# Two changes of order and of PSUM use in the FFN of a two-layer trunk on Trainium2

## The chip, the core and the metric

One core of a Trainium2 chip (trn2) runs the whole step as one program. The time is the device time of that core in microseconds, the median over repeated runs. TensorE (PE) does the products, VectorE (DVE), ScalarE (ACT) and GpSimd (POOL) what stands between them, SyncE (SP) issues the loads.

## The reference

`reference()` is one inference step of a trunk of two layers. Each layer is a half-step SwiGLU FFN, a token mixer (three head groups) and a second half-step FFN. The change lies in the FFN alone:

```python
def _ffn_half(x, mod, slot, w1, w3, w2, g, b):
    h = _modulate(x, mod[:, 3 * slot], mod[:, 3 * slot + 1])
    f = (jax.nn.silu(h @ w1) * (h @ w3)) @ w2
    return _residual_post_norm(x, f, mod[:, 3 * slot + 2], FFN_RES, g, b)
```

There are 640 tokens (128 of context, 512 latent), a model width of 1024 (8 tiles of 128 rows, called d0 to d7 here) and a hidden width of 2816 (22 tiles). Everything is float32.

## The kernel before

The activations lie transposed: a tile holds 128 features by 640 tokens. A float32 product is made of three fast ones: every operand is split into a high part (`hh`, `gh`, `wh`) and the small rest (`hl`, `gl`, `wl`), and high by high, high by low and low by high are summed in PSUM.

**One FFN** (function `ffn`; four calls, called FFN 1 to 4 here) goes over the 22 hidden tiles in six chunks of 3, 3, 3, 4, 4 and 4. The first three hidden tiles are computed plainly. Each of the other 19 is a `Pair`: the columns of w1 and of w3 for this hidden tile are stacked as a matrix of two by two blocks, the activations as another (features 0 to 511 and 512 to 1023, tokens 0 to 319 and 320 to 639), and the product is taken by a seven-product scheme, p1, p2, p4, p6, p7, p5, p3 in this order, each of 12 matmuls of 128x320 (L847) into one PSUM bank. The operands that are sums of blocks come from two places: of the activations (`t1` to `t4`) once per FFN, of the weights (`s1` to `s4`) on POOL for each pair (`combine`, L259). After a product's matmuls, `prod` calls `slot()`, which runs the follow-up steps put into the list `later`; a step that returns another step has that one run at the next slot. So a result of a product is read one product later or more. The steps: ACT copies p1 into `pm` (L895), DVE adds p2, p6, p7, p4, p5 and p3 to it in turn (`op`, L858), ACT takes the silu (L863, L877), DVE multiplies the two halves (L858, L881), and `hi` and `lo` split the product into `gh` (ACT, L886) and `gl` (DVE, L891). For the last pair of a chunk the first half of the tokens is split earlier, by `half` (L477, L478).

**The end of a chunk.** When the pairs are done, the remaining steps in `later` are issued, and the chunk's part of the product with w2 begins: eight feature tiles, each 3 matmuls for each hidden tile of the chunk and each part of the tokens (256 and 384 columns, L485), into `o`. Two tiles are begun (`begun`) with all hidden tiles but the last, whose `gh` is not there yet; `end_begun` then adds the last. `rows` does the others, and for each `resid` (DVE, L610) adds the result to the residual `x`, and `each()` may issue a step of the modulation vectors (`scr`, DVE L460, in FFN 1 to 3 only). The last chunk goes to `rows_norm` instead, which also takes the layer norm.

**PSUM.** Two buffers are double (two banks, `dbl`), four are single (`bank`). Buffers of a kind are used in turn, and the first matmul into one waits for the last reader of what it held.

**The weights** come through `Stream`, in the order in which `get` asks for them. A job is a half of a tile's load: SP loads the raw tile into one of two buffers (`wr`, L243), ACT makes the high part (`wh`, L299), DVE or POOL the low part (`wl`, L306). `get` converts ahead, as many jobs as fit in SLOTS (6) buffers, and the low part of a job is issued with `lows()` when the next job is converted. So the place of a `wl` in DVE's order is set by the calls of `get` around it, and a raw buffer comes free, and its next load can start, when the `wl` that reads it has been done.

What sets the work's order on each engine is then the order in which the Python code issues instructions.

```python
                while later:
                    slot()
                begun = []
                for d in range(2):
                    w = ws.get()
                    p = dbl("o") if d == 0 else [bank("o"), bank("o")]
```

Of the kernel before, what the change touches and what calls it, by code (L numbers as in the profile page):

```python
# [7 lines left out]
F32 = mybir.dt.float32  # L8
# [97 lines left out]
def trunk_kernel(tc, I, O):  # L106
# [3 lines left out]
    with ExitStack() as es:  # L110
# [520 lines left out]
        def rows(acts, n, begun, each):  # L631

            end_begun(begun, acts, n)
            for d in range(KD):
                if d < len(begun):
                    p = begun[d][1]
                else:
                    w = ws.get()
                    p = dbl("o")
                    mm(p, w, acts, 0, n)  # L640
                    mm(p, w, acts, 1, n)
                resid(p, d, None)
                each()

# [185 lines left out]
        class Pair:  # L830


            def __init__(self, h, tb, last):
                self.last = last
                self.b11, self.b21, self.b22 = ([[a[:, c] for a in h[k]] for k in ks]
                                                for ks, c in ((range(4), slice(0, HN)), (range(4, 8), slice(0, HN)),
                                                              (range(4, 8), slice(HN, T))))
                self.t1, self.t2, self.t3, self.t4 = (Quarter(tb, i) for i in range(4))
                self.m, self.sl = u(pe_, f"pm{uid()}"), None

            def out(self):
                self.gh, self.gl = u(pe_, f"gh{uid()}", F32R), u(pe_, f"gl{uid()}", F32R)
                return self.gh, self.gl

            def mms(self, out, w, b, k):
                for i, (a, c) in enumerate(((0, 0), (0, 1), (1, 0))):
                    PE.matmul(out[:, :HN], w[a][:, k, :], b[k][c], start=k == 0 and i == 0, stop=k == 3 and i == 2)  # L847

            def prod(self, out, b, post=None, w=None):
                w = w or ws.get()  # L850
                for k in range(4):
                    self.mms(out, w, b, k)
                slot()
                if post:
                    later.append(post)
# [1 line left out]
            def op(self, o, a, b, f):  # L857
                V.tensor_tensor(out=o, in0=a, in1=b[:, :HN], op=f)  # L858

            def c11(self, p2):  # L860
                self.sl = u(pe_, f"sl{uid()}")
                self.op(self.sl[:, LO], self.m[:, LO], p2, ALU.add)
                return lambda: S.activation(self.sl[:, LO], self.sl[:, LO], AF.Silu) and None  # L863

            def gate1(self):
                self.op(self.g[:, LO], self.g[:, LO], self.sl, ALU.mult)
                return self.half if self.last else None

            def half(self):
                split(self.gh[:, LO], self.gl[:, LO], self.g[:, LO])  # L870

            def c12(self, p3):
                self.op(self.sl[:, HI], self.m[:, LO], p3, ALU.add)
                return self.silu2

            def silu2(self):
                S.activation(self.sl[:, HI], self.sl[:, HI], AF.Silu)  # L877
                return self.gate2

            def gate2(self):  # L880
                V.tensor_tensor(out=self.g[:, HI], in0=self.g[:, HI], in1=self.sl[:, HI], op=ALU.mult)  # L881
                return self.hi

            def hi(self):
                c = HI if self.last else slice(0, T)
                S.copy(self.gh[:, c], self.g[:, c])  # L886
                return self.lo

            def lo(self):
                c = HI if self.last else slice(0, T)  # L890
                V.tensor_tensor(out=self.gl[:, c], in0=self.g[:, c], in1=self.gh[:, c].bitcast(F32), op=ALU.subtract)  # L891

            def start(self):
                p1, p2 = bank("p1"), bank("p2")
                self.prod(p1, self.b11, lambda: S.copy(self.m[:, LO], p1[:, :HN]) and None)  # L895
                self.prod(p2, self.b21, lambda: self.c11(p2))

            def run(self, mods, begun=False):
                m, op = self.m, self.op
                if not begun:  # L900
                    self.start()
                mods(0)
                p45 = dbl("p4")
                p4, p5 = p45[:, 0, :], p45[:, 1, :]
                self.prod(p4, self.t4)
                p6 = bank("p6")
                self.prod(p6, self.t2, lambda: op(m[:, LO], m[:, LO], p6, ALU.add))
                mods(1)
                p7 = bank("p7")

                def u3():
                    op(m[:, HI], m[:, LO], p7, ALU.add)
                    self.g = u(pe_, f"gf{uid()}")
                    op(self.g[:, LO], m[:, HI], p4, ALU.subtract)
                    return self.gate1
                self.prod(p7, self.t3, u3)

                def u4():
                    op(self.g[:, HI], m[:, HI], p5, ALU.add)
                    op(m[:, LO], m[:, LO], p5, ALU.add)  # L920
                self.prod(p5, self.t1, u4)
                mods(2)
                p3 = bank("p3")
                self.prod(p3, self.b22, lambda: self.c12(p3))

            def run_first(self, mods, other, ts):

                m, op = self.m, self.op
                self.start()
                mods(0)  # L930
                other.start()
                p3 = bank("p3")
                self.prod(p3, self.b22, None, ws.get(4))
                w22 = ws.get(0)
                p45, p6, p7 = dbl("p4"), bank("p6"), bank("p7")
                p4, p5 = p45[:, 0, :], p45[:, 1, :]
                wq = [ws.get(0), ws.get(0), ws.get(2), w22]
                for k in range(4):
                    for o, w, b in zip((p5, p7, p6, p4), wq, (self.t1, self.t3, self.t2, self.t4)):
                        self.mms(o, w, b, k)  # L940
                    mods(k)
                    next(ts, 0)
                slot()

                def post():
                    self.g = u(pe_, f"gf{uid()}")
                    op(m[:, LO], m[:, LO], p6, ALU.add)
                    op(m[:, HI], m[:, LO], p7, ALU.add)
                    op(self.g[:, LO], m[:, HI], p4, ALU.subtract)
                    op(self.g[:, HI], m[:, HI], p5, ALU.add)  # L950
                    op(m[:, LO], m[:, LO], p5, ALU.add)
                    later.append(self.gate1)
                    return self.c12(p3)
                later.append(post)

        LO, HI = slice(0, HN), slice(HN, T)

# [58 lines left out]
        def ffn(l, f, h, first, nmod, nvec, norm, scale_x, tb, ts):  # L1016
# [29 lines left out]
            for ci, (j0, j1) in enumerate(CHUNKS):  # L1046
# [44 lines left out]
                while later:  # L1091
                    slot()
                begun = []
                for d in range(2):
                    w = ws.get()
                    p = dbl("o") if d == 0 else [bank("o"), bank("o")]
                    for half in range(2):
                        for k in range(n - 2 if ci == 0 else n - 1):
                            mmk(part(p, half), w, gs, half, k, k, n)
                    begun.append((w, p, n - 1))  # L1100
# [911 lines left out]
        for l in range(DEPTH):  # L2012
            for f in range(2):
                for j0, j1 in CHUNKS:
                    for j in range(j0, j1):
                        tw = [I["w13"][l, f, j, :, wi] for wi in range(2)]
                        if j < NC:
                            for wi in range(2):
                                ws.tile(tw[wi], (KD, P), "m" if 2 * j + wi == NOPEN else None)
                            continue  # L2020
                        r = ws.pair(*tw)
                        for nm in BLOCKS:
                            ws.block(nm, r)
                    for d in range(KD):
                        ws.tile(I["w2"][l, f, d, :, j0:j1], (j1 - j0, P), "t" if j1 == NFF and d >= KD - NTAIL else None)
                if f == 1:
                    break
                for i in (0, 1, 3):
                    ws.tile(I["wint"][l, i], (KD, P))
                for gi in range(2):  # L2030
                    for hf in range(2):
                        ws.tile(I["winn"][l, gi, hf], (4, 256), None if gi + hf else "m")
                for i in (2, 4, 5, 6, 7, 8, 9, 10, 11):
                    ws.tile(I["wint"][l, i], (KD, P))
                ws.tile(I["wqup"][l], (6, P))
                ws.tile(I["wkvup"][l], (4, P))
                for d in range(KD):
                    ws.tile(I["wo"][l, d], (KD, P), "t" if d >= KD - NTAIL else None)
# [161 lines left out]
```

## Time and profile before

| what | value |
|---|---|
| median of 3 runs | 2693.86 us (2693.51 to 2696.27) |
| the profiled execution's own time | 2705.26 us |
| its span, first to last instruction | 2703.3 us |
| mean granted TensorE clock | 0.976 |
| busy: PE, DVE, ACT, POOL | 95%, 77%, 43%, 46% of the span |

The profile is of one execution. The span is from its first to its last instruction, and its own time stands 2 us above it. A share of busy time is a mean over the whole span. The trace's timeline gives each instruction's start and length, and in brackets how long its engine was idle before it and what ended that. The four FFNs lie at about 50 to 505, 945 to 1372, 1425 to 1843 and 2280 to 2675 us.

### The profile page before, as it was taken

To read this page: it belongs to the slowest core of one execution; us is meant where nothing else is said; L and a number is where in the kernel's file an instruction comes from. 1 tells how busy PE (TensorE), PEld (TensorE's weight loads), DVE (VectorE), ACT (ScalarE), POOL (GpSimd) and SP (SyncE) were. 2 spreads that over 40 slices of the span, in tenths; PEclk is the share of its full clock that TensorE was granted. 3 is DMA by queue.
4 is the path that set the end of the run, shared out by engine and by line. 5 is a ranking of instruction groups with operands and counts; after the bars stand their busy time and mean duration, and the time that the engine had idled before them with its cause. 6 is when DMAs were issued, how large, how long until landed. Compare 5 with 4: busy or idle time off the path is not lost. (4 is left out here: it accounts for less than half of the span.)

```text
span 2703.3 us, 49877 instructions
## 1 busy us (share of the span) xinstructions
PE 2555.0 (95%) x18662; PEld 2453.0 (91%) x18662; DVE 2072.3 (77%) x3759; ACT 1175.9 (43%) x2596; POOL 1244.0 (46%) x973
## 2 busy tenths in 40 slices
PE   7999999899999999999989999998998999999997
PEld 6999999888778999999989999998887798999997
DVE  6599889856764879988987998898476558777776
ACT  5233333545575533333353333334545745334333
POOL 2345445522444554544555454454233456435545
PEclk9999999999999999999989999998999999999998
DMA  7333332354344223333222333323543331222222
GB/s 273 116 98 101 111 97 83 117 152 136 91 130 156 71 96 100 103 101 109 68 83 84 112 103 101 110 87 108 158 134 98 103 114 40 82 82 87 79 86 71
DMA packets 130545, 285.89 MB, mean 106 GB/s; under 512 B 16832, under 2 KB 34560, under 8 KB 129664
## 3 DMA queue, kind: packets, MB, share of 16 engines
q1 hardware_dynamic: 130304, 282.70, 33.2%
q8 instruction: 148, 2.42, 0.4%
q14 instruction: 93, 0.76, 0.1%
HBM read 254.95 MB, written 8.81 MB: 98 GB/s over the span
## 5 line engine op out<-in xcount | busy, mean ns | idle before, releaser
L306 DVE TENSOR_TENSOR wl<-wr,wh 128x512 fp32r<-128x512 f32 (+1 forms) x524 | 518.3, 1003 | 74.1 <-ACT wh L299 72.5
L299 ACT CAST wh<-wr 128x512 fp32r<-128x512 f32 (+1 forms) x570 | 333.3, 607 | 479.4 <-DMA wr<-in_w 296.9
L485 PE MATMUL o<-gh,wh 128*128 128x256 f32 (+1 forms) x1408 | 439.5, 312 | 19.4 <-ACT gh L886 11.7
L485 PE MATMUL o<-gl,wh 128*128 128x256 f32 (+1 forms) x1408 | 439.0, 312 | 1.8 <-DVE gl L478 0.3
L485 PE MATMUL o<-gh,wl 128*128 128x256 f32 (+1 forms) x1408 | 436.7, 310 | 0.0
L847 PE MATMUL p<-hh,wh 128*128 128x320 f32 x1216 | 378.4, 311 | 16.8 <-DVE pm L858 16.8
L847 PE MATMUL p<-hl,wh 128*128 128x320 f32 x1216 | 378.2, 311 | 6.2 <-DVE hl L1010 6.2
L847 PE MATMUL p<-hh,wl 128*128 128x320 f32 x1216 | 378.1, 311 | 0.0
L259 POOL TENSOR_TENSOR ws<-wr 128x512 f32<-128x512 f32 x76 | 111.5, 1468 | 545.8 <-DMA wr<-in_w 482.8
L299 ACT CAST wh<-ws 128x512 fp32r<-128x512 f32 x304 | 185.9, 621 | 361.6 <-PE p L847 153.4
L306 POOL TENSOR_TENSOR wl<-ws,wh 128x512 fp32r<-128x512 f32 x152 | 241.3, 1591 | 193.6 <-ACT wh L299 193.1
L610 DVE SCALAR_TENSOR_TENSOR x<-o,gat,x 128x128 f32<-128x128 f32 (+2 forms) x404 | 192.9, 524 | 139.6 <-PE o L485 136.6
L485 PEld LDWEIGHTS o<-gh,wh 128*128 128x128 f32 x1408 | 267.8, 190 | 23.0 <-ACT gh L886 14.5
L485 PEld LDWEIGHTS o<-gl,wh 128*128 128x128 f32 x1408 | 268.1, 190 | 6.7 <-DVE gl L891 4.8
L485 PEld LDWEIGHTS o<-gh,wl 128*128 128x128 f32 x1408 | 267.9, 190 | 0.0
L847 PEld LDWEIGHTS p<-hh,wh 128*128 128x128 f32 x1216 | 229.9, 189 | 19.0 <-issue 18.9
L847 PEld LDWEIGHTS p<-hl,wh 128*128 128x128 f32 x1216 | 230.0, 189 | 7.4 <-DVE hl L1010 7.4
L847 PEld LDWEIGHTS p<-hh,wl 128*128 128x128 f32 x1216 | 230.0, 189 | 0.3 <-DVE wl L306 0.3
L460 DVE SCALAR_TENSOR_TENSOR scr<-wv,cb 128x512 f32<-128x512 f32 x192 | 181.2, 944 | 0.0
L259 POOL TENSOR_TENSOR ws<-wr,wr 128x512 f32<-128x512 f32 x76 | 130.2, 1713 | 0.0
L259 POOL TENSOR_TENSOR ws<-wr,ws 128x512 f32<-128x512 f32 x76 | 129.9, 1709 | 0.0
L259 POOL TENSOR_TENSOR ws<-ws,wr 128x512 f32<-128x512 f32 x76 | 119.1, 1567 | 6.0
(434 smaller groups left out, 6633.9 us busy)
## 6 DMA issues: line engine op xcount, KB each, us to landing
wr<-in_w SPq DMA_DIRECT2D x176, 512.0 KB, 4.2
wm<-in_wmod SPq DMA_DIRECT2D x192, 256.0 KB, 3.9
wr<-in_w SPq DMA_DIRECT2D x128, 256.0 KB, 2.7
wv<-in_wmt SPq DMA_DIRECT2D x96, 256.0 KB, 4.0
wr<-in_w SPq DMA_DIRECT2D x64, 192.0 KB, 2.4
wr<-in_wint SPq DMA_DIRECT2D x24, 512.0 KB, 4.2
wr<-in_wo SPq DMA_DIRECT2D x16, 512.0 KB, 3.8
xd<-x SPq DMA_DIRECT2D x16, 320.0 KB, 5.1
```

The costliest lines, as they stand in the source:

```text
L259: G.tensor_tensor(out=o, in0=x0, in1=x1, op=op)
L299: S.copy(hl[0], src[:, c0:c1])
L306: eng.tensor_tensor(out=t2, in0=src, in1=t.bitcast(F32), op=ALU.subtract)
L460: V.scalar_tensor_tensor(out=scr, in0=w[2 * i + hf], scalar=1.0, in1=cb[:, 2 * st + hf, :], op0=ALU.mult, op1=ALU.mult, accum_out=a[:, 2 * ...
L485: PE.matmul(out[:, :cn], whl[a][:, k, :], b[:, c0:c0 + cn], start=k == 0 and i == 0, stop=k == n - 1 and i == 2)
L610: V.scalar_tensor_tensor(out=c, in0=src, scalar=gat[:, d, s:s + 1], in1=c, op0=ALU.mult, op1=ALU.add)
L847: PE.matmul(out[:, :HN], w[a][:, k, :], b[k][c], start=k == 0 and i == 0, stop=k == 3 and i == 2)
```

## The change

1. The stacked matrix is made with its rows in the other order: `ws.pair(*tw[::-1])`, w3 above w1. Then p2 completes the linear half (`gf`, first tokens) and p4, p5, p6, p7 the silu half (`sl`); p3 completes the linear half of the other tokens, and the multiplication and the split follow. The silus are taken earlier, and after p3 one step fewer lies on ACT. The steps are written as closures in `run`; `run_first`, which nothing calls, is left out, and the steps' order in `later` is changed with them.
2. p6 and p7 are the halves of one double buffer, as p4 and p5 are.
3. In all chunks but the last three feature tiles are begun: d0 and d2 in double buffers, d1 in two single banks. d3 then takes two single banks. For d1 and d2 `ws.get` is told how far to convert (`SLOTS - 1 - d`), which is no further than d0's call got.

The core of the diff:

```diff
@@ rows
-                    p = dbl("o")
-                    mm(p, w, acts, 0, n)
-                    mm(p, w, acts, 1, n)
+                    p = [bank("o"), bank("o")] if d == 3 and len(begun) == 3 else dbl("o")
+                    for half in range(2):
+                        for k in range(n):
+                            mmk(part(p, half), w, acts, half, k, k, n)
...
@@ Pair
-            def c11(self, p2):
-                self.sl = u(pe_, f"sl{uid()}")
-                self.op(self.sl[:, LO], self.m[:, LO], p2, ALU.add)
-                return lambda: S.activation(self.sl[:, LO], self.sl[:, LO], AF.Silu) and None
...
-            def c12(self, p3):
-                self.op(self.sl[:, HI], self.m[:, LO], p3, ALU.add)
-                return self.silu2
...
+                def c11():
+                    self.g = u(pe_, f"gf{uid()}")
+                    op(self.g[:, LO], m[:, LO], p2, ALU.add)
+                self.prod(p1, self.b11, lambda: S.copy(m[:, LO], p1[:, :HN]) and None)
+                self.prod(p2, self.b21, c11)
                 mods(0)
-                p45 = dbl("p4")
-                p4, p5 = p45[:, 0, :], p45[:, 1, :]
+                p45, p67 = dbl("p4"), dbl("p6")
+                p4, p5, p6, p7 = (p[:, i, :] for p in (p45, p67) for i in range(2))
                 self.prod(p4, self.t4)
-                p6 = bank("p6")
                 self.prod(p6, self.t2, lambda: op(m[:, LO], m[:, LO], p6, ALU.add))
                 mods(1)
...
+                def c21():
+                    self.sl = u(pe_, f"sl{uid()}")
                     op(m[:, HI], m[:, LO], p7, ALU.add)
-                    self.g = u(pe_, f"gf{uid()}")
-                    op(self.g[:, LO], m[:, HI], p4, ALU.subtract)
-                    return self.gate1
-                self.prod(p7, self.t3, u3)
+                    op(self.sl[:, LO], m[:, HI], p4, ALU.subtract)
...
+                def c12():
+                    op(self.g[:, HI], m[:, LO], p3, ALU.add)
+                    self.gate(HI)
+                    return lambda: self.split(HI if self.last else slice(0, T))
+                self.prod(p3, self.b22, c12)
...
@@ ffn
-                for d in range(2):
-                    w = ws.get()
-                    p = dbl("o") if d == 0 else [bank("o"), bank("o")]
+                for d in range(2 if ci == len(CHUNKS) - 1 else 3):
+                    w = ws.get(SLOTS - 1 - d if d and ci < len(CHUNKS) - 1 else None)
+                    p = [bank("o"), bank("o")] if d == 1 else dbl("o")
...
-                        r = ws.pair(*tw)
+                        r = ws.pair(*tw[::-1])
```

**Where instructions move.** The examples are the end of FFN 2's second chunk (three hidden tiles). DVE there, before; `wl` are the low parts of the weights of d4, d5 and d6 in this order, `x` the residual's tiles of d0, d1 and d2 (a tile in two single banks has three rows):

```order
L306 TENSOR_TENSOR wl2387_12267<-wr2380_12241,wh2386_12266 128x384 [waits DMAHW1_49]
L306 TENSOR_TENSOR wl2390_12295<-wr2385_12264,wh2389_12294 128x384 [waits DMAHW2_49,Activation_49]
L610 SCALAR_TENSOR_TENSOR x2047_10292<-o2391_12297,gat_148,x2047_10292 128x512 [waits PE_49]
L610 SCALAR_TENSOR_TENSOR x2047_10292<-o2391_12297,gat_148,x2047_10292 128x128
L610 SCALAR_TENSOR_TENSOR x2048_10294<-o2395_12316,gat_148,x2048_10294 128x256
L610 SCALAR_TENSOR_TENSOR x2048_10294<-o2396_12317,gat_148,x2048_10294 128x256 [waits PE_49]
L610 SCALAR_TENSOR_TENSOR x2048_10294<-o2396_12317,gat_148,x2048_10294 128x128
L463 SCALAR_TENSOR_TENSOR mod1_145<-va2341_12060,const_108 128x2
L460 SCALAR_TENSOR_TENSOR scr2288_11797,va2397_12348<-wv2309_11907,cb2165_11114 128x512
L306 TENSOR_TENSOR wl2394_12314<-wr2388_12292,wh2393_12313 128x384 [waits DMAHW3_49,Activation_49]
L610 SCALAR_TENSOR_TENSOR x2049_10296<-o2402_12358,gat_148,x2049_10296 128x512 [waits PE_49]
```

and with the change, some rows further on: `wl` of d5, d6 and d7, the residual of d3, `wl` of the next pair's block a11, the residual of d4:

```order
L460 SCALAR_TENSOR_TENSOR scr2274_11789,va2378_12350<-wv2295_11898,cb2151_11105 128x512 [waits DVE_49]
L306 TENSOR_TENSOR wl2373_12284<-wr2368_12252,wh2372_12283 128x384 [waits DMAHW2_49,Activation_49]
L306 TENSOR_TENSOR wl2382_12361<-wr2371_12281,wh2381_12360 128x384 [waits DMAHW3_49,Activation_49]
L306 TENSOR_TENSOR wl2385_12367<-wr2380_12358,wh2384_12366 128x384 [waits DMAHW5_49,Activation_49]
L610 SCALAR_TENSOR_TENSOR x2036_10289<-o2388_12373,gat_148,x2036_10289 128x256 [waits PE_49]
L610 SCALAR_TENSOR_TENSOR x2036_10289<-o2389_12374,gat_148,x2036_10289 128x256 [waits PE_49]
L610 SCALAR_TENSOR_TENSOR x2036_10289<-o2389_12374,gat_148,x2036_10289 128x128
L460 SCALAR_TENSOR_TENSOR scr2274_11789,va2378_12350<-wv2327_12052,cb2151_11105 128x512 [waits DVE_49]
L306 TENSOR_TENSOR wl2387_12371<-wr2383_12364,wh2386_12370 128x512 [waits DMAHW6_49,Activation_49]
L610 SCALAR_TENSOR_TENSOR x2037_10291<-o2393_12403,gat_148,x2037_10291 128x512 [waits PE_49]
```

Before, d5's `wl` stands ahead of the residuals of d0 and d1, and d6's, d7's and a11's each behind a residual of its own. Now d5's stands behind the residuals of d0 to d2, and d5's, d6's and d7's follow each other ahead of d3's residual.

PE at the same place, before: the last two matmuls of p3, then the first of d0, which waits for ACT's `wh` (its own weights):

```order
L847 MATMUL p32384_12262<-hl2114_10598,wh2365_12158 128x320
L847 MATMUL p32384_12262<-hh2113_10597,wl2366_12159 128x320
L485 MATMUL o2391_12297<-gh2294_11832,wh2368_12177 128x256 [waits Activation_49]
L485 MATMUL o2391_12297<-gl2295_11833,wh2368_12177 128x256
L485 MATMUL o2391_12297<-gh2294_11832,wl2369_12178 128x256 [waits DVE_49]
```

and with the change, where d0's first matmul waits for DVE as well. That wait is for the instruction that adds p7 to `pm`, since d0 now takes the double buffer of p6 and p7:

```order
L850 MATMUL p32367_12250<-hl2100_10589,wh2349_12150 128x320
L850 MATMUL p32367_12250<-hh2099_10588,wl2350_12151 128x320
L485 MATMUL o2374_12286<-gh2280_11824,wh2353_12170 128x256 [waits DVE_49,Activation_49]
L485 MATMUL o2374_12286<-gl2281_11825,wh2353_12170 128x256
L485 MATMUL o2374_12286<-gh2280_11824,wl2354_12171 128x256
```

The double buffer of d6, with the change; the wait on DVE is for the residual of d4, which had the buffer before:

```order
L485 MATMUL o2397_12430<-gl2344_12126,wh2372_12283 128x384
L485 MATMUL o2397_12430<-gh2343_12125,wl2373_12284 128x384
L485 MATMUL o2406_12468<-gh2280_11824,wh2381_12360 128x256 [waits DVE_49,PE_49,Activation_49]
L485 MATMUL o2406_12468<-gl2281_11825,wh2381_12360 128x256
L485 MATMUL o2406_12468<-gh2280_11824,wl2382_12361 128x256
```

The order of the tiles on PE is the same as before; what each waits for has moved.

## Rows read from the trace of the kernel before

**Rows 1.** The page, parts 1 and 2: busy times; granted clock in 40 slices.

```profile
PE 2555.0 (95%) x18662; PEld 2453.0 (91%) x18662; DVE 2072.3 (77%) x3759; ACT 1175.9 (43%) x2596; POOL 1244.0 (46%) x973
...
PEclk9999999999999999999989999998999999999998
```

**Rows 2.** Waits of PE: line waited for, us in total, times, longest us.

```profile
PE p L847 <- DVE pm L858: 16.8, 8, 3.5
...
PE o L485 <- ACT gh L886: 11.7, 13, 1.1
```

**Rows 3.** Stretches: PE, PEld, DVE, ACT, POOL busy (count), granted clock, DMA.

```profile
350.00:400.00 50.00, 46.48 (x300) 46.25 (x300) 44.97 (x72) 19.30 (x37) 20.51 (x13) 0.93 0.29 86
...
1200.00:1250.00 50.00, 48.20 (x326) 47.71 (x325) 47.42 (x71) 20.06 (x38) 30.85 (x19) 1.00 0.30 100
...
2350.00:2400.00 50.00, 50.00 (x344) 50.00 (x342) 35.03 (x61) 18.22 (x35) 21.82 (x15) 1.00 0.24 75
```

**Rows 4.** Timeline (start, us, ..., [idle before]), PE, end of FFN 2's second chunk.

```profile
1036.19 0.28 PE L485 MATMUL o<-gh,wh 128*128 128x256 f32 x1
...
1041.95 0.45 PE L485 MATMUL o<-gh,wh 128*128 128x384 f32 x1 [1.05 <-ACT gh L886]
...
1059.28 0.31 PE L847 MATMUL p<-hh,wh 128*128 128x320 f32 x1
```

**Rows 5.** Timeline, DVE, the same chunk end.

```profile
1035.89 0.48 DVE L858 TENSOR_TENSOR pm<-pm,p 128x320 f32<-128x320 f32 x1
...
1042.34 1.02 DVE L306 TENSOR_TENSOR wl<-wr,wh 128x384 fp32r<-128x384 f32 x2
1043.28 2.04 DVE L610 SCALAR_TENSOR_TENSOR x<-o,gat,x 128x512 f32<-128x512 f32 x5
...
1045.98 0.56 DVE L306 TENSOR_TENSOR wl<-wr,wh 128x384 fp32r<-128x384 f32 x1
1046.45 1.00 DVE L610 SCALAR_TENSOR_TENSOR x<-o,gat,x 128x512 f32<-128x512 f32 x2
1047.37 0.68 DVE L460 SCALAR_TENSOR_TENSOR scr<-wv,cb 128x512 f32<-128x512 f32 x1
```

**Rows 6.** Timeline, ACT, the same chunk end: casts of d6 and d7, then of a11.

```profile
1045.39 1.05 ACT L299 CAST wh<-wr 128x384 fp32r<-128x384 f32 x2 [3.08 <-DMA wr<-in_w]
1051.21 1.14 ACT L299 CAST wh<-wr 128x512 fp32r<-128x512 f32 x2 [4.76 <-DMA wr<-in_w]
```

**Rows 7.** Timeline, PE, end of FFN 4's second chunk.

```profile
2368.38 0.28 PE L485 MATMUL o<-gh,wh 128*128 128x256 f32 x1
...
2389.45 0.31 PE L847 MATMUL p<-hh,wh 128*128 128x320 f32 x1
```

**Rows 8.** Timeline, DVE, the same chunk end of FFN 4.

```profile
2371.76 1.02 DVE L306 TENSOR_TENSOR wl<-wr,wh 128x384 fp32r<-128x384 f32 x2
...
2375.46 0.56 DVE L306 TENSOR_TENSOR wl<-wr,wh 128x384 fp32r<-128x384 f32 x1
```

**Rows 9.** Timeline, ACT, the same chunk end of FFN 4.

```profile
2374.92 0.97 ACT L299 CAST wh<-wr 128x384 fp32r<-128x384 f32 x2 [3.18 <-DMA wr<-in_w]
2380.06 1.14 ACT L299 CAST wh<-wr 128x512 fp32r<-128x512 f32 x2 [4.17 <-DMA wr<-in_w]
```

**Rows 10.** Timeline, DVE, end of FFN 2's fourth chunk: p7 read.

```profile
1173.59 0.48 DVE L858 TENSOR_TENSOR pm<-pm,p 128x320 f32<-128x320 f32 x1
```

**Rows 11.** Timeline, PE, first matmul of d0 at that chunk end.

```profile
1172.52 0.28 PE L485 MATMUL o<-gh,wh 128*128 128x256 f32 x1
```

**Rows 12.** Timeline, PE, inside FFN 2's fourth chunk: first matmul of a p2.

```profile
1161.89 0.39 PE L847 MATMUL p<-hh,wh 128*128 128x320 f32 x1 [1.94 <-DVE pm L858]
```

**Rows 13.** Timeline, DVE, the same place: reads of p6, p7 and p5.

```profile
1161.27 0.47 DVE L858 TENSOR_TENSOR pm<-pm,p 128x320 f32<-128x320 f32 x1
...
1162.95 0.47 DVE L858 TENSOR_TENSOR pm<-pm,p 128x320 f32<-128x320 f32 x1
...
1165.34 0.48 DVE L858 TENSOR_TENSOR pm<-pm,p 128x320 f32<-128x320 f32 x1
```

More of the change, by code (lines that the diff above doesn't have):

```diff
@@ L838, in __init__ @@
                 self.t1, self.t2, self.t3, self.t4 = (Quarter(tb, i) for i in range(4))
-                self.m, self.sl = u(pe_, f"pm{uid()}"), None
+                self.m = u(pe_, f"pm{uid()}")
             def out(self):
@@ L843, in out, with prod @@
                 return self.gh, self.gl
[L845 to L850, printed above, removed]
+            def prod(self, out, b, post=None):
+                w = ws.get()
                 for k in range(4):
-                    self.mms(out, w, b, k)
+                    for i, (a, c) in enumerate(((0, 0), (0, 1), (1, 0))):
+                        PE.matmul(out[:, :HN], w[a][:, k, :], b[k][c], start=k == 0 and i == 0, stop=k == 3 and i == 2)
                 slot()
@@ L858, in op @@
                 V.tensor_tensor(out=o, in0=a, in1=b[:, :HN], op=f)
-            def c11(self, p2):
-                self.sl = u(pe_, f"sl{uid()}")
-                self.op(self.sl[:, LO], self.m[:, LO], p2, ALU.add)
-                return lambda: S.activation(self.sl[:, LO], self.sl[:, LO], AF.Silu) and None
[L865 to L870, printed above, removed]
@@ L872, in c12 @@
-            def c12(self, p3):
-                self.op(self.sl[:, HI], self.m[:, LO], p3, ALU.add)
-                return self.silu2
[L876 to L885, printed above, removed]
-                S.copy(self.gh[:, c], self.g[:, c])
-                return self.lo
@@ L889, in lo, with gate @@
[L889 to L893, printed above, removed]
-                p1, p2 = bank("p1"), bank("p2")
[L895 to L901, printed above, removed]
+            def gate(self, c):
+                V.tensor_tensor(out=self.g[:, c], in0=self.g[:, c], in1=self.sl[:, c], op=ALU.mult)
@@ new lines, in split, with lo, run @@
+            def split(self, c):
+                S.copy(self.gh[:, c], self.g[:, c])
+                def lo():
+                    V.tensor_tensor(out=self.gl[:, c], in0=self.g[:, c], in1=self.gh[:, c].bitcast(F32), op=ALU.subtract)
+                return lo
+            def run(self, mods):
+                m, op = self.m, self.op
+                p1, p2 = bank("p1"), bank("p2")
+                def c11():
[3 more added lines that the diff above has]
+                self.prod(p2, self.b21, c11)
@@ L902, in run @@
                 mods(0)
-                p45 = dbl("p4")
-                p4, p5 = p45[:, 0, :], p45[:, 1, :]
+                p45, p67 = dbl("p4"), dbl("p6")
+                p4, p5, p6, p7 = (p[:, i, :] for p in (p45, p67) for i in range(2))
                 self.prod(p4, self.t4)
-                p6 = bank("p6")
                 self.prod(p6, self.t2, lambda: op(m[:, LO], m[:, LO], p6, ALU.add))
                 mods(1)
-                p7 = bank("p7")
-                def u3():
+                def c21():
+                    self.sl = u(pe_, f"sl{uid()}")
@@ L912, in u3, with silu @@
                     op(m[:, HI], m[:, LO], p7, ALU.add)
-                    self.g = u(pe_, f"gf{uid()}")
-                    op(self.g[:, LO], m[:, HI], p4, ALU.subtract)
-                    return self.gate1
-                self.prod(p7, self.t3, u3)
-                def u4():
-                    op(self.g[:, HI], m[:, HI], p5, ALU.add)
+                    op(self.sl[:, LO], m[:, HI], p4, ALU.subtract)
+                    def silu():
+                        S.activation(self.sl[:, LO], self.sl[:, LO], AF.Silu)
+                        return gate1
@@ L920, in u4, with gate1, c22 @@
+                    return silu
+                def gate1():
+                    self.gate(LO)
+                    return (lambda: self.split(LO)) if self.last else None
+                self.prod(p7, self.t3, c21)
+                def c22():
+                    op(self.sl[:, HI], m[:, HI], p5, ALU.add)
                     op(m[:, LO], m[:, LO], p5, ALU.add)
-                self.prod(p5, self.t1, u4)
+                    return lambda: S.activation(self.sl[:, HI], self.sl[:, HI], AF.Silu) and None
@@ L922, in run @@
+                self.prod(p5, self.t1, c22)
                 mods(2)
                 p3 = bank("p3")
[L924 to L954, printed above, removed]
```

## The prediction

> **What bounds the kernel.** I read the page first: PE is busy 95% of the span, at a granted clock of nearly full speed in all 40 slices; DVE, the next, 77% [rows 1]. So time comes and goes only where PE stands still, or where its clock falls after it did. The waits of PE come next: 16.8 us in 8 waits of products for DVE's `pm`, and 11.7 us in 13 waits of w2's matmuls for ACT's `gh` [rows 2]. These two are what the change works on. Then stretches: in FFN 2 DVE is busy 47.42 of 50 us, in FFN 4, which has no `scr`, 35.03, and there PE is busy for the whole 50 [rows 3]. DVE is the engine behind both waits, wherever it is nearly full. Last, the timeline of chunk ends, with and without a wait.
>
> **1. The wait for `gh` goes.** At the end of FFN 2's second chunk, d0's first matmul starts at 1036.19, PE waits 1.05 us for `gh`, and the next product starts at 1059.28: 23.09 us for eight tiles [rows 4]. The same work without a wait, in FFN 4, takes 2389.45 - 2368.38 = 21.07 us, 2.63 a tile [rows 7]. So the wait of 1.05 costs 2.02 us: matmuls next to it run longer (0.45 us instead of 0.34 for the first [rows 4]). The third begun tile puts 2/3 of 2.63 = 1.8 us (3/4 in chunks of four tiles) between d0 and the need for `gh`, and a step on ACT is gone; both cover the 1.05. Gain: between 11.7, the idle time alone, and 11.7 x 2.02/1.05 = 22.5. I take 20, near the upper end, since that is what the whole stretch shows. **-20.**
>
> **2. d0 waits for p7 to be read.** d0 now takes the banks of p6 and p7. In FFN 2's second chunk that read runs from 1035.89 to 1036.37 [rows 5], d0's first matmul started at 1036.19 [rows 4]: 0.2 us late. In its fourth chunk the read ends at 1174.07 [rows 10], d0 started at 1172.52 [rows 11]: 1.55. I read the two times at all 24 ends: in 12 of them, all in FFN 1 to 3, the read is later, by amounts like these two. With their mean of 0.87 that is 10; the twelve themselves gave 8.7, and I take **+8**. Bounds: 0, if DVE's new order reads p7 sooner, and 16, if each 1 us costs 2 as in part 1.
>
> **3. d6 waits for a residual that waits for a load.** Every tile from d4 on takes a double buffer, so d6 needs that of d4, freed by d4's residual. DVE's new order (shown above) has `wl` of d5, d6, d7, then the residual of d3, `wl` of a11, then the residual of d4. A raw buffer is free when its `wl` is done: d7's load starts after d5's `wl`, a11's after d6's. Before, these `wl` were spread, and early: d5's was done at 1043.4 (the second of two from 1042.34), before the residual of d0, and d6's at 1046.54 [rows 5]. Now d5's stands behind d2's residual. How long from the end of a `wl` to the cast of the load it set free? d7: the second `wl` of FFN 4 ends at 2372.8 [rows 8], the second cast starts at 2375.4 (the pair began at 2374.92, one takes 0.5) [rows 9]: 2.6 us. a11: 2376.02 [rows 8] to 2380.06 [rows 9], 4.04; in FFN 2 1046.54 [rows 5] to 1051.21 [rows 6], 4.67.
>
> For FFN 2's second chunk: d0 starts at 1036.4, the three begun tiles are finished 3 x 2.63 later, at 1044.3. d2's residual and a `scr` end DVE's work of before at about 1047.7; d5's `wl` (0.5) ends at 1048.2. d7's cast starts at 1048.2 + 2.6 = 1050.8, its `wl` ends at 1051.9; residual of d3 (1.0) and a `scr` (0.7) follow; a11's load, free since 1048.7, is cast at 1053.4, its `wl` ends at 1054.7, and d4's residual at 1055.7. PE wants d6 three tiles after 1044.3, at 1052.2: a stall of 3.5 us. In FFN 4 DVE has no `scr` and comes to d5's `wl` at once; by the same steps the residual of d4 ends 1.65 us after PE wants d6. In chunks of four hidden tiles a feature tile takes 4/3 of 2.63, 0.9 us more, so PE gives 2.6 more up to d6, while the load of d7, a third larger, takes up to 0.9 longer (if the whole 2.6 grows by a third): 3.5 - 2.6 is 0.9, with the load 1.8. I take 1.0 us in FFN 1 to 3, none in FFN 4. The first chunk's loads come early; none. Sum, over chunks 2 and 3 and then 4 and 5 of FFN 1 to 3, and two ends of FFN 4: 6 x 3.3 (3.0 to 3.65 between the latencies above) + 6 x 1.0 + 2 x 1.65 = **+29**. Bounds: 0, if the loads land before DVE stands at them; 45, if d7 is late as well by half as much.
>
> **4. Products inside a chunk: 0.** Before, p2 waits for the read of p6: 1.94 us [rows 12], after a read that ends at 1161.74 [rows 13]. Joined, p6 and p7 go to the next pair's p4 and p5 turn and about: p4 waits for the read of p7, p6 for the last read of p5. The p7 read here ends at 1163.42 [rows 13]; without its wait p2 would start at 1159.8, p4 one product (12 x 0.147 = 1.76) later, at 1161.5: it waits 2.0. The p5 read ends at 1165.82 [rows 13], p6 could start at 1165.3: 0.6 more. DVE's backlog is the same; the wait moves by one product. Bounds: -16.8, all of the row [rows 2], and +6 for the 0.6 at eight places and some more. I take 0.
>
> A rule speaks against my 0. The Trainium skill, Perfetto Trace Analysis, section "Identifying Performance Opportunities", says that a gap which repeats on the engine that should be full can mean that PSUM or SBUF lacks room for the next tile. By it, the other use of the banks would take the eight waits away, and the sum below would be +6, not +23. It is the third rival.
>
> **5. The clock.** In the stretch with the 3.5 us wait the granted clock is 0.93; in one of FFN 2 where PE stood for 1.8 us (50 less 48.20) it is 1.00 [rows 3]. A fall to 0.93 of 50 us is 3.5 us. Six of the new waits are of about 3.3 us; I add 1 us each, **+6** (0 to 18).
>
> The silus and additions that change places (row order, closures) are as many as before, on the same engines: nothing by themselves. Split on POOL, loads and their sizes are unchanged.
>
> **Sum:** -20 + 8 + 29 + 0 + 6 = **+23 us**. The profiled execution took 2705.3 with its 2703.3 span, 11.4 us (0.4%) over the median; I let that difference stand: 2728 profiled, **2717** as a median. A difference under 0.2%, 5.4 us, can't be told from none.
>
> **Rivals.**
> *A: DVE doesn't stand at the loads* (chance 0.20). If d7 and a11 are in place when DVE comes to them, part 3 is 0 and -20 + 8 = -12 stays: 2682. It decides where d4's residual ends before 1052.2 in the example, 3.5 us sooner than worked out. For it: PE's tiles are finished later if d0 waits, and DVE is 35.03 of 50 us busy in FFN 4 [rows 3]. Against: the chain of two loads lies in DVE's own order, and its latencies are read at the same place [rows 5 to 9].
> *B: the new waits drop the clock* (0.12). If each us of them costs two as in part 1, part 3 is 56, part 2 16: -20 + 16 + 56 = +52, 2746. For: 0.93 after 3.5 us [rows 3]. Against: most new waits lie a little below that one. The Trainium skill, TensorE: Matmul & The Clock Gate, section "Why this matters for your kernels", asks that no gaps be left between bursts of matmuls, as throughput drops after them; the row at 0.93 agrees, the one at 1.00 shows that not every gap does it.
> *C: the repeated wait inside the chunks goes as well* (0.15). Part 4 is then between -16.8 and -32, with 2.02/1.05 as in part 1: 23 - 16.8 to 23 - 32, or 2700 to 2685, about no change. Against: the read of p7 comes as late for p4 as that of p6 did for p2 [rows 12, 13].
>
> **How the numbers follow.** My forecast has 0.53: slower by over 0.2% in 0.49 of it, since with the lower latencies and no clock term it is still +10 or so; no change 0.04. A: faster 0.20. B: slower 0.12. C: no change 0.10, faster 0.03, slower 0.02. Together faster 0.23, same 0.14, slower 0.63. The range runs from 2676, which takes in A's plain case and leaves out A with the gain of C (0.08), to 2738, which takes in the upper latencies of part 3 and leaves out most of B (0.10). The forecast's own range is 2703 to 2738.
>
> **What would show it.** In the waits of PE the row of `gh` is gone; a new one of `o` for DVE's residual `x` L610 stands at 20 to 35 us, the longest about 3.5; `p` for DVE's sums stays near 17. In the waits of DVE, `wl` for ACT's `wh` grows. In the timeline of FFN 2's second chunk d6's first matmul waits 3 us or more, and its eight tiles take about 25 us. No wait at d6 makes the prediction wrong on part 3; no wait in the products makes it wrong on part 4.

## The result, and the profile after

The changed kernel takes 2727.78 us (median of 4 runs, 2721.51 to 2734.4), the kernel before 2695.07 in the runs beside it: a ratio of 1.0116, interval 1.0085 to 1.0147. It is slower by about 32 us; 2717 was predicted, and the sign and the range held.

The profiled execution of the changed kernel took 2721.51 us, its span 2719.7; it is the quickest of its four runs, while that of the kernel before (2705.26) lay above its runs' median, so the two traces differ by 16 us only (26 us more in the four FFNs, some 9 less in the rest). I compare waits in the traces and times in the ratios.

The waits of PE for DVE and for ACT, over the whole span (columns as in [rows 2]):

```profile
PE o L485 <- DVE x L610: 28.2, 18, 3.0
PE o L485 <- DVE pm L856: 23.2, 13, 2.9
...
PE p L850 <- DVE wl L306: 2.1, 2, 1.0
```

Both rows of [rows 2] are gone: there is no row of w2's matmuls for `gh`, and none of the products for `pm`. Two new ones stand there, and they are larger: d6 and its like waiting for a residual, 28.2 us, and d0 waiting for the read of p7, 23.2 us.

The end of FFN 2's second chunk, PE, answers to [rows 4]:

```profile
1039.73 0.36 PE L485 MATMUL o<-gh,wh 128*128 128x256 f32 x1 [0.39 <-DVE pm L856]
...
1052.98 0.28 PE L485 MATMUL o<-gh,wh 128*128 128x256 f32 x1
...
1058.74 0.55 PE L485 MATMUL o<-gh,wh 128*128 128x256 f32 x1 [2.96 <-DVE x L610]
1059.09 0.41 PE L485 MATMUL o<-gl,wh 128*128 128x256 f32 x1
...
1063.67 0.41 PE L485 MATMUL o<-gh,wh 128*128 128x256 f32 x1
...
1066.86 0.31 PE L850 MATMUL p<-hh,wh 128*128 128x320 f32 x1
```

1039.73 is d0, 1052.98 d5, 1058.74 d6 after its wait, 1063.67 d7, 1066.86 the next product: 27.13 us for the eight tiles, against 23.09 before, 21.07 without a wait [rows 4, 7] and the 25 or so that were forecast. Two things are to be seen. PE stands for 2.96 us before d6. And then d6 itself takes 4.93 us, to 1063.67, where d5 took 5.76 with the wait of 2.96 in it, that is 2.8: a matmul of 256 columns shows 0.41 us where it showed 0.28.

DVE over the same time, to be read against [rows 5]:

```profile
1044.93 0.55 DVE L306 TENSOR_TENSOR wl<-wr,wh 128x384 fp32r<-128x384 f32 x1
1046.87 2.05 DVE L610 SCALAR_TENSOR_TENSOR x<-o,gat,x 128x512 f32<-128x512 f32 x5 [1.39 <-PE o L485]
...
1051.11 1.02 DVE L306 TENSOR_TENSOR wl<-wr,wh 128x384 fp32r<-128x384 f32 x2
1054.61 0.56 DVE L306 TENSOR_TENSOR wl<-wr,wh 128x384 fp32r<-128x384 f32 x1 [2.48 <-ACT wh L299]
1055.08 1.13 DVE L610 SCALAR_TENSOR_TENSOR x<-o,gat,x 128x256 f32<-128x256 f32 x3
...
1056.98 0.69 DVE L306 TENSOR_TENSOR wl<-wr,wh 128x512 fp32r<-128x512 f32 x1 [0.16 <-ACT wh L299]
1057.59 1.00 DVE L610 SCALAR_TENSOR_TENSOR x<-o,gat,x 128x512 f32<-128x512 f32 x2
```

and ACT, against [rows 6]:

```profile
1054.06 0.51 ACT L299 CAST wh<-wr 128x384 fp32r<-128x384 f32 x1 [5.58 <-DMA wr<-in_w]
1056.33 1.14 ACT L299 CAST wh<-wr 128x512 fp32r<-128x512 f32 x2 [1.75 <-DMA wr<-in_w]
```

At 1051.11 DVE does the `wl` of d5 and d6. It then stands 2.48 us for d7's, whose cast stood for its load: from the end of d5's `wl`, 1051.66, to the cast at 1054.06 are 2.4 us. The residual of d3 follows, then a11's `wl`, then d4's residual from 1057.59, whose first and larger part frees nothing until its second ends at 1058.59; d6 starts at 1058.74. DVE idles while PE waits for DVE.

### The profile page after: what moved, and what is told of

Same layout as the page of the kernel before. It is cut to its first block, busy times and chain, and to the rows that moved or that the text cites. A ratio compares the mean times of both kernels' runs of the same rounds, so it can differ in the third digit from the quotient of the medians.

```text
span 2719.7 us, 49890 instructions
## 1 busy us (share of the span) xinstructions
PE 2547.8 (94%) x18662; PEld 2445.3 (90%) x18662; DVE 2024.9 (74%) x3779; ACT 1178.3 (43%) x2596; POOL 1238.8 (46%) x973
## 5 line engine op out<-in xcount | busy, mean ns | idle before, releaser
L306 DVE TENSOR_TENSOR wl<-wr,wh 128x512 fp32r<-128x512 f32 (+1 forms) x524 | 507.3, 983 | 120.8 <-ACT wh L299 120.3
L485 PE MATMUL o<-gh,wh 128*128 128x384 f32 (+1 forms) x1408 | 445.5, 316 | 56.8 <-DVE x L610 27.8
L485 PE MATMUL o<-gl,wh 128*128 128x384 f32 (+1 forms) x1408 | 441.0, 313 | 0.0
L485 PE MATMUL o<-gh,wl 128*128 128x384 f32 (+1 forms) x1408 | 440.6, 313 | 0.0
L460 DVE SCALAR_TENSOR_TENSOR scr<-wv,cb 128x512 f32<-128x512 f32 x192 | 170.8, 889 | 0.0
L856 DVE TENSOR_TENSOR pm<-pm,p 128x320 f32<-128x320 f32 x228 | 109.0, 478 | 47.4 <-PE p L850 47.4
L259 POOL TENSOR_TENSOR ws<-ws,wr 128x512 f32<-128x512 f32 x76 | 125.0, 1645 | 6.0
L306 DVE TENSOR_TENSOR wl<-ws,wh 128x512 fp32r<-128x512 f32 x152 | 127.5, 851 | 0.0
```

The source lines that it names most:

```text
L259: G.tensor_tensor(out=o, in0=x0, in1=x1, op=op)
L306: eng.tensor_tensor(out=t2, in0=src, in1=t.bitcast(F32), op=ALU.subtract)
L460: V.scalar_tensor_tensor(out=scr, in0=w[2 * i + hf], scalar=1.0, in1=cb[:, 2 * st + hf, :], op0=ALU.mult, op1=ALU.mult, accum_out=a[:, 2 * ...
L485: PE.matmul(out[:, :cn], whl[a][:, k, :], b[:, c0:c0 + cn], start=k == 0 and i == 0, stop=k == n - 1 and i == 2)
```

## The experiments

Two questions were open: are the two new waits caused where I put them, at the order of the `wl` and at the double buffer of p6 and p7; and are they causes at all, or one backlog of DVE that is paid wherever PE first asks for it? In the first four runs parts of the change are taken out, or d6's wait is.

**Row order alone.** From the changed kernel, p6 and p7 are put back into single banks and two tiles begun:

```diff
-                p45, p67 = dbl("p4"), dbl("p6")
-                p4, p5, p6, p7 = (p[:, i, :] for p in (p45, p67) for i in range(2))
+                p45 = dbl("p4")
+                p4, p5 = p45[:, 0, :], p45[:, 1, :]
...
+                p6 = bank("p6")
...
+                p7 = bank("p7")
...
-                for d in range(2 if ci == len(CHUNKS) - 1 else 3):
-                    w = ws.get(SLOTS - 1 - d if d and ci < len(CHUNKS) - 1 else None)
+                for d in range(2):
+                    w = ws.get()
```

> The change with only the rows' order kept: p6 and p7 in two single banks as before, two feature tiles begun, as before. Theory (the new waits come from the double buffer of p6 and p7 and from the third begun tile): no wait of the first w2 matmul for pm, no wait of o for the residual x; the waits of products for pm stay near 17 us; the wait for gh goes or falls under 3 us, as one ACT step is gone. So 10 to 20 us faster than before, about 2680. Rival (the row order itself makes DVE late): waits of 10 us or more for pm or x stay, and the time is that of before or above.

Measured: 1.0014 (1.0002 to 1.0026), 2701.09 us where 2680 was expected. Its waits of PE:

```profile
PE o L485 <- ACT gh L863: 16.0, 14, 2.2
...
PE p L850 <- DVE pm L856: 8.8, 7, 1.7
PE o L485 <- DVE gl L866: 7.8, 15, 0.5
```

The theory was half wrong. d0 and d6 don't wait, as it said. But the products' wait, which was to stay near 17, is halved from 16.8, and the wait for `gh` grew from 11.7 to 16.0, with 7.8 for `gl` behind it. The matmul that waits is now that of the first tokens, not of the last:

```profile
1179.63 0.39 PE L485 MATMUL o<-gh,wh 128*128 128x256 f32 x1 [2.16 <-ACT gh L863]
```

In the old order the first half of the hidden tile was split early (`half`), only the second late. With the new one both silus end late, and with two begun tiles PE is there first. So the row order shortens the last chain by a step and lengthens the one before it. (The section on the change says that the silus are taken earlier. That holds for the last tokens; the first tokens' silu stood behind p2 before and stands behind p7 now.)

**Row order and the double buffer,** with the second half of the edit above alone (two begun).

> Row order and the double buffer of p6 and p7, but two feature tiles begun with the calls of get as before. Theory: the products' wait for pm is gone, as in the changed kernel, and is paid at d0's first matmul instead, some 15 to 25 us; no wait of o for the residual x over 3 us. About the time of before, 2685 to 2700. Rival (joining really takes the products' wait away, and d0's wait belongs to the third begun tile): d0 waits under 8 us in all and the time is under 2680.

Measured: 1.0012 (0.9999 to 1.0024), 2702.75 us.

```profile
PE o L485 <- DVE pm L856: 24.4, 15, 2.6
...
PE o L485 <- DVE gl L866: 3.1, 6, 0.5
...
PE p L850 <- DVE pm L856: 1.8, 4, 0.5
PE o L485 <- ACT gh L863: 0.9, 4, 0.3
```

As the theory said, but for a time a little above its 2685 to 2700. The products' wait is gone (1.8), d0's wait of 24.4 has come, and it covers most of the waits for `gh` and `gl`, 23.8 in the run above, now 4.0. Together these rows are 30.2 us here and 32.6 in the run above; a wait of the products for `wl`, 4.2 us, is new. The time is the same.

**Row order and three begun tiles,** with the first half of the edit alone (single banks).

> Row order and three feature tiles begun, but p6 and p7 in two single banks. Theory: the wait of o for the residual x stays near 28 us, the products' wait for pm comes back near 17, d0's wait for pm is gone; 2710 to 2725. Rival (one DVE backlog, paid at whichever wait comes first, so that the joined buffer decides d6 too): x under 15 us.

Measured: 1.0061 (1.0043 to 1.0079), 2715.2 us.

```profile
PE o L485 <- DVE x L610: 27.7, 16, 4.4
...
PE p L850 <- DVE pm L856: 4.9, 5, 1.9
PE o L485 <- ACT gh L863: 1.8, 2, 0.9
```

d6's wait is that of the changed kernel, 27.7 against 28.2, without the double buffer: it belongs to the third begun tile and what `get` does there. The products' wait was expected near 17 and is 4.9: it is the row order that lowers it, not the buffer alone.

**The conversions spread out.** The changed kernel, with one line of `rows` altered:

```diff
-                    w = ws.get()
+                    w = ws.get(3 if len(begun) == 3 and d < 6 else None)
```

> The changed kernel, but from d3 to d5 get converts one job at a time, so that the low parts of d6, d7 and a11 stand behind the residuals of d3, d4 and d5 and not all ahead of d3's and d4's. Theory (d6 waits because d4's residual stands behind low parts that wait for loads): the wait of o for the residual x falls from 28.2 us to under 6, the clock falls after it go as well; 25 to 38 us faster than the changed kernel, 2690 to 2703; d0's wait for pm stays at 20 to 28. Rival (DVE is simply behind with its work there): 15 us or more of that wait stay.

Measured: 1.0076 (1.0056 to 1.0097), 2716.84 us, some 11 us faster than the changed kernel by the ratios (0.0040 of 2697; the intervals leave 10 either way, and the two traces differ by 7.9) and not 25.

```profile
PE o L485 <- DVE pm L856: 30.5, 13, 3.0
...
PE p L850 <- POOL wl L306: 9.4, 6, 1.8
...
PE o L485 <- DVE x L610: 0.4, 2, 0.2
```

d6's wait is gone, 28.2 to 0.4, so the place of the conversions (each `wl`, and the cast ahead of it) is its cause. Of the gain 7.3 us went to d0's wait and 9.4 to a new one: the next pair's blocks are converted too late. The spreading was too strong. The next runs use a weaker one, `ws.get(4 if len(begun) == 3 and d < 5 else None)`, which puts d7's `wl` behind d3's residual and a11's behind d4's.

**d0 in single banks.** The changed kernel, d0 and d1 exchanged in their buffers:

```diff
-                    p = [bank("o"), bank("o")] if d == 1 else dbl("o")
+                    p = [bank("o"), bank("o")] if d == (1 if ci == len(CHUNKS) - 1 else 0) else dbl("o")
```

> The changed kernel, but d0 takes the two single banks and d1 the double buffer of p6 and p7. Theory (d0 waits for the read of p7 because of that buffer): the first w2 matmul no longer waits for pm; 23.2 us fall to under 6, what is left at d1, one tile later; d6's wait for x stays at 25 to 32. 12 to 20 us faster than the changed kernel, 2708 to 2716. Rival (DVE's backlog is a debt that is paid at the next wait whatever the buffer): the waits of o for gh, gl or x grow by 10 us or more, and the time is within 6 us of the changed kernel.

Measured: 1.0020 (1.0006 to 1.0033), 2702.02 us.

```profile
PE o L485 <- DVE x L610: 26.7, 16, 4.1
PE o L485 <- DVE pm L856: 7.6, 5, 2.4
...
PE p L850 <- DVE pm L856: 0.8, 2, 0.5
```

15.6 us of the wait for `pm` go and nothing takes their place: there is no row for `gh`, as the third begun tile covers it. What is left, 7.6 where under 6 was expected, is nearly all in three waits of 2.3 to 2.4 at the last chunk of FFN 1, 2 and 3, where this edit leaves d0 in the double buffer. By the ratios the gain is 0.0096, 26 us (the intervals leave some 9 either way), more than the 12 to 20 expected and more than the wait. The two profiled executions differ by 15.5 us, as the wait does; that of the changed kernel is the quickest of its four, and that of this run the slowest of its ten, so the other 10 us don't show in these traces.

**The weaker spreading,** alone.

> The changed kernel with get told to convert only 4 jobs ahead at d3 and d4. Theory: d6's wait for x falls from 28.2 to under 6 as with the stronger spreading, and the products' wait for POOL's wl (9.4 us there, as the next pair's blocks were converted too late) stays under 4; d0's wait for pm 25 to 32. 2700 to 2712. Rival (the later the residuals the later everything): POOL's wl waits as long as there and the time is 2716 or more.

Measured: 1.0057 (1.0038 to 1.0076), 2712.06 us: 16 us faster than the changed kernel (the intervals leave 10 either way).

```profile
PE o L485 <- DVE pm L856: 30.3, 15, 2.9
...
PE o L485 <- DVE x L610: 4.3, 11, 0.6
...
PE p L850 <- POOL wl L306: 0.4, 1, 0.4
```

POOL's `wl` is in time; d0's wait is 30.3 as with the stronger spreading.

**Both mends,** the weaker spreading and d0 in single banks.

> Both mends: d0 in the single banks, and get told to convert only 4 jobs ahead at d3 and d4. Theory (both waits are the price of placement, not of work): waits of o for pm under 6 and for x under 6, no wait for gh over 3; 2680 to 2695, faster than the kernel before by 0.1 to 0.7%. Rival (a debt that only moves): 10 us or more of waits come up elsewhere, and the time is 2697 or more.

Measured: **0.9960** (0.9943 to 0.9976), 2685.48 us: faster than the kernel before, and 42 us faster than the changed one. The two mends gave 26 and 16 alone: within the intervals they add up.

```profile
PE o L485 <- DVE pm L856: 9.6, 10, 2.4
...
PE o L485 <- DVE x L610: 3.2, 10, 0.7
```

From 51.4 us in the changed kernel these two rows are down to 12.8. Under 6 was expected of the first, and 9.6 are left: three waits of 2.3 to 2.4 make most of it, again at the last chunk of FFN 1, 2 and 3.

**Single banks, three begun, weaker spreading:** the run with three begun tiles above and the line of `rows`.

> Row order and three tiles begun, p6 and p7 in single banks, and get told to convert only 4 jobs ahead at d3 and d4, so that the low part of a11 stands behind d4's residual and that of d7 behind d3's. Theory: of the 27.7 us of d6's wait for x under 5 are left; products wait for pm 5 us as without the spreading; 15 to 25 us faster than with three begun and single banks alone: 2688 to 2700, that is the time of before or up to 0.4% less. Rival (freed time is lost again at the next chunk's first weights): waits of products for wl of 8 us or more.

Measured: 0.9967 (0.9952 to 0.9981), 2687.89 us. d6's wait is 5.7 us and the products' 7.0, a little over the 5 expected of each, and `gh` is 3.4. The intervals of this version and of the last overlap: with the third tile and the spreading, joining p6 and p7 and moving d0 out of their buffer gains nothing that was measured. Joining them and leaving d0 there costs: the weaker spreading alone is this version with that buffer, and stands at 1.0057.

**The old row order.** The kernel before, with three begun tiles and the spreading as the only changes.

> The kernel before with only the third begun tile and get told 4 jobs ahead at d3 and d4: rows in the old order, p6 and p7 in single banks. What is asked: is the row order needed. Theory 1 (the third tile alone covers gh, the row order gains nothing): wait for gh under 3 us, products' wait for pm near 17 us as before, x under 7; 2680 to 2691. Theory 2 (the row order takes half of the products' wait away and is worth it): the products' wait is 17 us or more and the time is 2693 or more, above the same kernel with the new row order (2687.89).

Measured: 0.9978 (0.9962 to 0.9994), 2692.94 us: between the two theories. The products' waits for DVE are 12.0 and 4.9 us (for `pm` and for `sl`), `gh` 2.3. The third tile by itself, placed well, beats the kernel before. Against the same with the new row order the intervals overlap, so what the row order adds stays open.

**Both mends, two begun tiles.**

> The faster version (d0 in single banks, joined p6 and p7, new row order), but with two begun tiles and the calls of get as before. Theory: the wait for gh comes back, 12 to 18 us, as with the row order alone, since the new order splits the first tokens' half later; d1's wait for pm up to 10; 2695 to 2705. Rival (the third tile isn't needed once d0 is free): gh under 5 us, 2680 to 2690.

Measured: 1.0022 (1.0011 to 1.0033), 2703.88 us.

```profile
PE o L485 <- ACT gh L863: 12.5, 10, 1.8
PE o L485 <- DVE pm L856: 7.6, 5, 2.4
...
PE o L485 <- DVE gl L866: 6.0, 12, 0.5
```

The spreading has no part here, as it acts only where three tiles are begun. With the new row order the third begun tile is what covers `gh`: without it the waits for `gh` and `gl` are back at 18.5 us, and the gain is gone.

## Why the prediction was right, and where it was not

First a correction: the chunks hold 4, 3, 3, 4, 4 and 4 hidden tiles, not 3, 3, 3, 4, 4 and 4 as the section on the kernel before says; the first has three plain tiles and one pair. The sums went by chunks 2 to 5 and don't change.

**Part 1, the wait for `gh`: right.** 11.7 us are gone, and with the short gaps for `gl` behind them, which the list of waits leaves out, some 17 to 19 from one matmul's start to the next; 20 was taken. But the two reasons I gave weigh differently. The third begun tile does it, in the old row order too (2.3 us left); the row order alone raised the wait to 16.0.

**Part 3, d6: right in cause and size.** +29 was forecast, and the row shows 28.2. Six ends of three hidden tiles in FFN 1 to 3 wait 2.78 to 3.00 us each (forecast 3.3), those of four tiles 0.77 to 0.84 and one 1.75 (1.0), FFN 4 two, of 1.26 and 2.75 (1.65 each). The chain was as worked out: 2.4 us from a `wl` to the cast of the load that it freed, where 2.6 was taken. The waits of DVE's `wl` for ACT's `wh` grew, as forecast, from 72.5 us to 120.3. The stronger spreading, which moved only the conversions, took d6's wait to 0.4. Rival A, in which DVE would not stand at the loads, did not happen.

**Part 2, d0: the place right, the size not.** I took +8 and bounded it by 16; the row shows 23.2. **Part 4, the products: wrong.** I took 0, since I let the wait move from p2 to p4; there is none left in the changed kernel.

Both sizes were read from the kernel before, on the premise that the additions and silus which change places do nothing by themselves. That is the step that failed, and the run with the row order alone shows it, in which no banks are joined. The products' wait falls to 8.8 there, and p7 is read later. Counted as in part 2 at all 24 ends (how far the end of the read lies behind the end of p3's matmuls, where it does), the read is late by 8.7 us before, by 23.4 with the row order alone, by 20.4 with three tiles and single banks, by 23.4 in the changed kernel, and by 11.1 with the third tile in the old row order. At the fourth chunk of FFN 2, p7's read and d0 with the row order alone:

```profile
1174.81 0.48 DVE L856 TENSOR_TENSOR pm<-pm,p 128x320 f32<-128x320 f32 x1
```

```profile
1172.03 0.28 PE L485 MATMUL o<-gh,wh 128*128 128x256 f32 x1
```

The read ends 3.26 us late, where before it was 1.55 [rows 10, 11], but d0 stands in another buffer and waits for nothing. The same read in the changed kernel:

```profile
1176.72 1.28 DVE L306 TENSOR_TENSOR wl<-wr,wh 128x512 fp32r<-128x512 f32 x2
...
1180.83 0.69 DVE L306 TENSOR_TENSOR wl<-wr,wh 128x512 fp32r<-128x512 f32 x1 [2.43 <-ACT wh L299]
1181.44 0.48 DVE L856 TENSOR_TENSOR pm<-pm,p 128x320 f32<-128x320 f32 x1
```

and PE:

```profile
1182.06 0.36 PE L485 MATMUL o<-gh,wh 128*128 128x256 f32 x1 [2.85 <-DVE pm L856]
```

The read stands behind a `wl`, and this behind a load, and d0, now in the joined buffer, waits 2.85 for it.

In sum -16.8 for the products and +15.2 more at d0 than forecast nearly cancel. That brought the total out right, and it is luck as far as the runs show, for this is not one cost at two places. With three begun tiles and single banks the products wait 4.9 us and d0 not at all; joining p6 and p7 on top of that puts 23.2 us at d0, and 0.0055, some 15 us, on the time (the intervals leave 10 either way); with the weaker spreading on both sides it is 0.0090, some 24 us. With two begun tiles joining looks free only since d0's wait there covers those for `gh` and `gl`. And with d0 in other banks 15.6 us of the wait went and nothing took their place. How much of the read's lateness comes from the steps' new order on DVE, and how much from PE no longer standing inside the chunk while DVE catches up, no run separates: with the row order alone the products wait 8.0 us less, and the read is 14.7 us later.

The Trainium skill's rule on repeated gaps (Perfetto Trace Analysis, "Identifying Performance Opportunities"), by which the other use of the banks would take the eight waits away, came true for the eight, half of which the row order took away before it (16.8 to 8.8, joined 1.8), and not for the time (rival C): a larger gap stood at d0.

**Part 5, the clock: right.** +6 was taken. There are ten waits above 2.7 us at the chunks' ends, seven at d6 and three at d0; after four of them, all at d6, the tiles ran slower. By chunk (time of the eight tiles over that without a wait, less the idle time) these four cost 1.9, 3.1, 1.8 and 3.0 us, 9.8 together; after the other six the granted clock stayed at 1.00. It also fell after three shorter waits at d0 (2.33, 2.54 and 2.30 us), and in the kernel before after waits that are gone now. Net, matmuls at the lower clock cost 15.6 us in the four FFNs before and 20.2 with the change: +4.6. Rival B, a fall after every wait, did not happen.

Counted from one matmul's start to the next, so that gaps are a little longer than in the list of waits, the parts are -18 (`gh` and `gl`), +25 (d0), +30 (d6), -19 (products for DVE's sums), +2 (products for `wl`) and +5 (the clock), together +25. That is near the +23 of the forecast, and near the 26 us by which the four FFNs are longer in the trace (the matmuls' own time taken off: 98 us lost, before 72). The ratio gives 32; which of the other 6 to 8 us are part of the change and which are scatter of the runs (2721.51 to 2734.4) was not settled.

## What to carry to other kernels

Where a queue of small steps of one engine frees both the buffers of the next loads and the banks of the next products, its order is a resource: a step that waits for a load must not stand ahead of one that frees a bank, and a request for data further ahead can put it there. A lateness that is read from a profile in order to price a new wait holds for the order of steps in that profile: here the reordering of a few additions and silus alone, with as many of them as before, took one read from 8.7 us late in sum to 23.4. And start the next stage in a buffer whose last reader is done: exchanging two names took 15.6 us of waits away here, and 26 us by the ratios.

## What the runs showed of the chip

Waits of the same length are not followed by the same clock. After the 2.96 us at 1058.74 PE was granted half its clock, 1.2 of 2.4 GHz, for about 6 us (stretches; PEclk is the granted clock):

```profile
core 0: us, PE busy (x) PEld busy (x) DVE busy (x) ACT busy (x) POOL busy (x), PEclk, DMA share, GB/s
1055.00:1060.00 5.00, 2.04 (x11) 1.75 (x10) 4.84 (x12) 1.44 (x3) 0.27 (x1) 0.81 0.54 178
1060.00:1065.00 5.00, 5.00 (x21) 5.00 (x21) 4.33 (x7) 1.52 (x3) 4.92 (x4) 0.51 0.00 0
```

After a wait of 2.96 us at the third chunk end of FFN 1 the clock stayed at 1.00 (the wait in the timeline, then the stretch around it):

```profile
254.33 0.35 PE L485 MATMUL o<-gh,wh 128*128 128x256 f32 x1 [2.96 <-DVE x L610]
```

```profile
252.00:260.00 8.00, 5.67 (x39) 5.71 (x40) 8.00 (x18) 2.61 (x5) 5.17 (x4) 1.00 0.17 64
```

I had not expected that two waits equal to a hundredth of a us differ so. In the first, PE shows as busy for 5 of 5 us at 0.51, with 21 matmuls in the stretch where 1040 to 1045 has 36 at 1.00. Nor is a short wait safe: in the kernel before, a wait of 1.06 us for `gh` at 1102.24 lies in a stretch at 0.67, while the like wait at 1041.95 [rows 4] has no fall behind it. A sum of waits by line shows the idle time alone; the slower matmuls behind a wait must be read from windows.

```profile
1102.00:1106.00 4.00, 3.68 (x16) 3.42 (x17) 3.78 (x10) 0.91 (x3) 0.00 (x0) 0.67 0.38 114
```

DVE is behind nearly all of these waits, and part of its lateness comes with POOL's work. In the kernel before, ahead of the read of p6 for which p2 waits 1.94 us [rows 12, 13], DVE needs 1.90 us for a `gl`, and POOL works all that time. A pair later POOL is idle, and the same takes 0.82:

```profile
1159.45 1.90 DVE L891 TENSOR_TENSOR gl<-gf,gh 128x640 fp32r<-128x640 f32 x1
...
1170.09 0.82 DVE L891 TENSOR_TENSOR gl<-gf,gh 128x640 fp32r<-128x640 f32 x1
```

```profile
1158.94 3.54 POOL L306 TENSOR_TENSOR wl<-ws,wh 128x512 fp32r<-128x512 f32 x2
```

Over that trace such a `gl` takes 0.82 us where POOL is idle throughout and 1.75 where it is busy throughout (25 of each), the product of the two halves (128x320) 0.49 and 1.48, and the additions from PSUM into `pm` 0.48 either way. No run moved POOL's work, so what that would do to PE's waits is open.
